# Context pieces beside light experts only, and a new order of the experts

## The chip, the cores and the metric

The kernel runs on one core of a Trainium2 chip. The metric is the device time of one execution in microseconds, as the median of several runs. Engines are named as in the profile: PE (TensorE), PEld (its weight loads), DVE (VectorE), ACT (ScalarE), POOL (GpSimd) and SP (SyncE, which here issues most of the transfers from HBM).

## What is computed

Two model blocks follow each other. The first is a mixer and a mixture of 32 experts; the second has two layers that attend jointly to 512 tokens and to a context of 256 tokens. The change touches the expert stage of the first block. Its core, cut from the reference:

```python
logits = (xf @ w_router).astype(jnp.float32) + b_router.astype(jnp.float32)
top_val, top_idx = lax.top_k(logits, TOP_K)          # 4 of 32 experts a token
...
hu = xb @ w_up[e] + b_up[e]
x_glu = jnp.minimum(hu[:, :D_FF], SWIGLU_LIMIT)
x_lin = jnp.clip(hu[:, D_FF:], -SWIGLU_LIMIT, SWIGLU_LIMIT)
act = x_glu * jax.nn.sigmoid(SWIGLU_ALPHA * x_glu) * (x_lin + 1.0)
return act @ w_down[e] + b_down[e]
```

So each expert has three matrices of 1024 x 1024 float32 values, 4 MB each: the gate half of w_up, the linear half of w_up, and w_down. The context's part of the second block's first layer does not depend on the first block:

```python
hc, gate_c = adaln(xc, mod_c)
qac, kac, vac, qbc, kbc, vbc, gc = heads_ab(hc @ w_in, *wts)
...
mixc = jnp.concatenate([oac, obc], axis=-1) * jax.nn.silu(gc)
xc = xc + gate_c * (mixc @ w_out)
```

It is therefore computed beside the experts.

## The kernel before

The experts are ranked by their number of tokens. `CAPS` gives the places of each rank: ranks 0 and 1 have two blocks (128 and 64 tokens, called T here), ranks 2 to 13 have one of 128 (heavy, H), ranks 14 to 31 one of 64 (light, L). `moe` (line 780) makes a list `order` of ranks and works through it. In iteration i it runs the gate matrix of expert i (`expert_gate`), then the w_down matrix of expert i-1 (`expert_down`), then the linear matrix of expert i (`expert_lin`). Ahead of the last it prepares the tokens of the expert after (`turn`) and the slots and the gather of the one after that (`prep`). One more iteration, i = 32, runs the last w_down.

`expert_mm` (line 1193) works on one matrix. It issues four transfers of 1 MB on SP's queue (line 1214, tile `raw`, four buffers for the whole stage). For a light expert it multiplies the float32 weights directly, 32 matmuls of 512 columns (line 1221), and ACT and DVE fold the two halves of the result afterwards (lines 1175 and 1176). For heavy and two-block experts every half of `raw` is split into a high part on ACT (line 72, `whi`) and a low part on DVE (line 73, `wlo`), in buffers of which there are four, and 48 matmuls of 512 columns follow (line 1236); a T expert has more of them for its second block. Line 1211 or 1219 starts the sums with the bias.

The context is the generator `context` (line 1476). Its 57 yields make 58 steps, here called pieces: 24 of projections and norms, 4 of queries, keys and values, 18 of attention, 8 of `w_out`, then the row normalization for the second layer and two pieces of that layer's keys and values. The matrix pieces load their weights on SP (line 1510), split them on ACT and DVE (lines 72 and 73), and run 24 matmuls of 256 columns (lines 98 to 100) each. `moe` calls `step()` behind each matrix, three times an iteration; each call lets the generator go on by one piece, until call 30, and from there three of four calls do. The order of the instructions on an engine is the order of the code with these pieces between; a scheduler then moves instructions a little.

The order before is L, then H L for ranks 13 to 2 (i = 1 to 24), then T L L (i = 25 to 27), T L L (28 to 30), and L (31). The context is used up by about i = 22. One iteration ahead of `last` (i = 23) the rest of the generator is drained, and a pool `moe3` for the token tiles of the last experts is opened in the place that the context's memory has left; `tags` names the token tiles, and `hilo` (line 1147) takes those named y and v from `moe3`.

Behind the loop the hook `after` prepares the second block (`second_start`, line 2063): gains and rows of scale factors are loaded on ACT's queue (lines 2043 to 2073), POOL makes the tables of rope gains (lines 1837 to 1844), and two weight tiles of the second block are loaded on SP (line 77). Then a branch (line 1329) skips the work for overfull experts, and `combine` (line 1376) loads the experts' rows (`y<-Yd`) and adds them; each row is normalized with its statistics on POOL (line 68) before the first matmul of the second block.

Of the kernel before, what the change touches and what calls it, by code (L numbers as in the profile page):

```python
# [13 lines left out]
BF16 = mybir.dt.bfloat16  # L14
# [7 lines left out]
P = 128  # L22
D = 1024
S = 512
NT = S // P
# [9 lines left out]
class Net:  # L35
# [737 lines left out]
    NE = 32  # L773
# [6 lines left out]
    def moe(self, mix, mods, close, x1, modd, h2d, Yd, bd, beside=(), after=None):  # L780
# [4 lines left out]
        NE = self.NE  # L785
        with ExitStack() as ctx:
# [24 lines left out]
            with c2:  # L811
                pools = self.moe_pools(c2)
                self.xg_init(pools)

                light = list(range(14, NE))
                order = [light.pop(0)]
                for r in range(13, -1, -1):
                    order += [r] + [light.pop(0) for _ in range(min(len(self.CAPS[r]), len(light)))]
                order += light

                last = min(i for i, r in enumerate(order) if len(self.CAPS[r]) > 1) - 1
                tags = []
                for i, r in enumerate(order):
                    if len(self.CAPS[r]) > 1:
                        tags.append("xz")
                    elif i >= last:
                        tags.append("v" if tags[-1] == "y" else "y")
                    elif self.CAPS[r] == (64,) and (not i or tags[-1] != "z"):
                        tags.append("z")
                    else:  # L830
                        tags.append("x")

                def prep(r, behind=None):
                    out, off = [], 0
# [29 lines left out]
                self.extra_plan(c1, tab)  # L864
                down, beside = None, iter(beside)

                cnt = [0]

                def step():
                    cnt[0] += 1  # L870
                    if cnt[0] < 30 or cnt[0] % 4:
                        next(beside, None)

                more = ExitStack()

                for i in range(NE + 1):
                    if i < NE:
                        r = order[i]
                        pk = pick[:, r : r + 1]
                        e = nc.values_load(tab["eri"][0:1, r : r + 1], engines=[mybir.EngineType.SP], min_val=0,  # L880
                                           max_val=NE - 1)
                        wu = A["w_up"][0, ds(e, 1)].rearrange("o k c -> (o k) c")
                        wd = A["w_down"][0, ds(e, 1)].rearrange("o k c -> (o k) c")
                        hs = self.expert_gate(raws, pools, tab, cur, pk, wu)
                        step()
                    if down is not None:
                        self.expert_down(raws, pools, tab, *down, Yd)
                        step()
                    if i < NE:
                        if i + 1 == last:  # L890
                            for _ in beside:
                                pass
                            pools["more"] = more.enter_context(self.pool("moe3", 1, side="right"))
                        nxt = turn(ahead, i + 1) if i + 1 < NE else None
                        ahead = prep(order[i + 2]) if i + 2 < NE else None
                        acts = self.expert_lin(raws, pools, tab, cur, hs, pk, wu)
                        down = (cur, acts, pk, wd)
                        cur = nxt
                        step()
                more.close()  # L900
                if after is not None:
                    after()
            self.moe_extra(tab, h2d, Yd)
# [194 lines left out]
    def slots(self, pools, tab, pos, rhs, cap, later=False):  # L1098
# [1 line left out]

        nc = self.nc
        t2 = pools["t2"]
        oh = t2.tile([P, NT, P], BF16, tag="oh", name="oh")
        iota = tab["iota_s"] if cap == 128 else tab["iota_d"]
        nc.vector.tensor_tensor(oh, iota[:, None, :].to_broadcast([P, NT, P]), pos.to_broadcast([P, NT, P]),
                                op=OP.is_equal)
# [40 lines left out]
    def hilo(self, pools, tag, cap, whole):  # L1147


        t2 = pools["more"] if tag in "yv" else pools["t2"]  # L1150
        x = {"whole": whole}
        if whole:
            x["f"] = t2.tile([P, KT, cap], F32, tag=tag + "h", name=tag, bufs=1)
# [1464 lines left out]
```

## Time and profile before

| what | value |
|---|---|
| median of 3 runs | 2619.11 us (2616.77 to 2623.46) |
| the profiled execution | 2624.55 us, its span 2622.8 us |
| PE busy | 2343.2 us, 89% of the span |
| PEld busy | 1594.3 us, 61% |
| DVE busy | 1661.4 us, 63% |
| ACT busy | 1150.0 us, 44% |
| POOL busy | 500.5 us, 19% |
| read from and written to HBM | 563.56 MB and 23.46 MB, 224 GB/s over the span |

The profile is of one execution. A busy PE is not PE at its peak, since the ends of matmuls are modelled; idle time of an engine that does not bound a stretch costs nothing. The expert loop runs from about 536 to 1889 us. What one change there is worth is read from its own stretch, not from the shares of the whole span. Times in all rows count from the start of the span.

### The profile page before, as it was taken

The page shows a single profiled execution, that of the slowest core. Times are in us where ns is not written, and L with a number is a line of the kernel's source. Part 1 is how long each engine was busy: PE and PEld are TensorE (multiplying, and loading weights), DVE is VectorE, ACT ScalarE, POOL GpSimd, SP SyncE. Part 2 cuts the span into 40 slices and gives each one's busy share as a digit, 9 for nine tenths or more (in the row PEclk, how much of TensorE's full clock was granted, in tenths as well). Part 3 has the DMA queues.
Part 4 walks back from the last instruction along what each step waited for, and adds up shares of the span by engine and source line. Part 5 has one row for each costly group of instructions (what it writes and reads, how often), then busy time and mean ns, then how long its engine had stood idle before and what let it go on. Part 6 is the DMA issues. An engine that isn't in the chain of part 4 may idle for free. (4 is left out here: it accounts for less than half of the span.)

```text
span 2622.8 us, 33292 instructions
## 1 busy us (share of the span) xinstructions
PE 2343.2 (89%) x12070; PEld 1594.3 (61%) x12070; DVE 1661.4 (63%) x2730; ACT 1150.0 (44%) x1948; POOL 500.5 (19%) x686
## 2 busy tenths in 40 slices
PE   4987998979999999999999989999659899999888
PEld 4864666636656555555556556454159787687766
DVE  6798564456566686667566765444286788556483
ACT  3342553224454455455445443333224478432362
POOL 4335332210010001011000000000143213232112
PEclk7998998999999999999999989999979899999999
DMA  7551204689999998898999998888962101222101
GB/s 259 180 174 65 98 17 148 239 314 322 344 335 324 333 350 298 317 331 312 346 353 341 339 336 314 296 309 303 370 223 78 40 33 33 89 76 89 67 22 41
DMA packets 207234, 580.85 MB, mean 221 GB/s; under 512 B 16739, under 2 KB 68944, under 8 KB 207066
## 3 DMA queue, kind: packets, MB, share of 16 engines
q1 hardware_dynamic: 186624, 539.33, 57.8%
q10 hardware_dynamic: 13210, 22.57, 2.5%
q0 software_dynamic: 7232, 16.79, 1.8%
q8 instruction: 96, 1.57, 0.2%
q14 instruction: 72, 0.59, 0.1%
HBM read 563.56 MB, written 23.46 MB: 224 GB/s over the span
## 5 line engine op out<-in xcount | busy, mean ns | idle before, releaser
L73 DVE TENSOR_TENSOR wlo<-raw,whi 128x1024 fp32r<-128x1024 f32 (+3 forms) x420 | 510.2, 1250 | 129.3 <-ACT whi L72 128.2
L72 ACT ACTIVATE whi<-raw 128x1024 fp32r<-128x1024 f32 (+4 forms) x439 | 462.8, 1093 | 201.0 <-PE ps L100 48.9
L1236 PE MATMUL ps<-whi,x 128*128 128x512 f32 x896 | 268.9, 412 | 12.3 <-ACT whi L72 12.3
L1176 DVE TENSOR_TENSOR fold<-ps,fold 64x512 f32<-64x512 f32 x120 | 82.0, 683 | 206.7 <-ACT fold L1175 205.0
L1236 PEld LDWEIGHTS ps<-whi,x 128*128 128x128 f32 x896 | 174.2, 197 | 61.8 <-ACT whi L72 21.4
L1221 PE MATMUL ps<-raw,z 128*64 128x512 f32 x768 | 187.6, 609 | 3.8 <-DMA raw<-in_w_up_dram 3.8
L1142 POOL DMA_INDIRECT xg<-h2d,si x34 | 40.6, 1193 | 652.2 <-issue 199.8
L1175 ACT ACTIVATE fold<-ps 64x512 f32<-64x512 f32 x120 | 71.1, 593 | 205.5 <-PE ps L1221 178.7
L1236 PE MATMUL ps<-wlo,x 128*128 128x512 f32 x448 | 154.1, 426 | 7.1 <-DVE wlo L73 6.6
L1221 PE MATMUL ps<-raw,a 128*64 128x512 f32 x576 | 139.0, 608 | 4.1 <-DMA raw<-in_w_down_dram 3.4
L73 DVE TENSOR_TENSOR PTl<-tp,PTh 128x512 fp32r<-128x512 f32 (+1 forms) x178 | 111.6, 639 | 46.3 <-ACT PTh L72 44.6
L1914 ACT ACTIVATE pt<-sp,st 128x768 f32<-128x768 f32 (+4 forms) x160 | 110.2, 690 | 57.7 <-DVE st L1908 24.2
L1908 DVE TENSOR_REDUCE st<-sp 128x1 f32<-128x768 f32 (+5 forms) x144 | 108.3, 753 | 42.6 <-PE sp L449 17.2
L1236 PE MATMUL ps<-whi,a 128*128 128x512 f32 x448 | 129.9, 402 | 1.1 <-ACT whi L72 1.1
L72 ACT ACTIVATE PTh<-tp 128x512 fp32r<-128x512 f32 (+1 forms) x178 | 97.4, 559 | 70.6 <-PE tp L1952 55.6
L1293 POOL DMA_INDIRECT Yd<-y,si x34 | 38.5, 1133 | 390.2 <-ACT y L1291 388.4
L1952 PE MATMUL tp<-ident,pt 128*128 128x128 f32 x648 | 107.2, 278 | 3.2 <-DVE QS L490 1.3
L73 POOL TENSOR_TENSOR wlo<-raw,whi 128x2048 fp32r<-128x2048 f32 (+2 forms) x19 | 76.5, 4033 | 148.2 <-ACT whi L72 132.9
L1236 PEld LDWEIGHTS ps<-wlo,x 128*128 128x128 f32 x448 | 81.4, 197 | 36.2 <-DVE wlo L73 20.2
L1236 PEld LDWEIGHTS ps<-whi,a 128*128 128x128 f32 x448 | 84.1, 190 | 21.4 <-ACT whi L72 1.6
L1221 PEld LDWEIGHTS ps<-raw,z 128*64 128x64 f32 x768 | 46.7, 136 | 79.6 <-issue 70.3
L1952 PEld LDWEIGHTS tp<-ident,pt 128*128 128x128 f32 x648 | 78.9, 142 | 22.7 <-issue 3.6
(728 smaller groups left out, 5400.9 us busy)
## 6 DMA issues: line engine op xcount, KB each, us to landing
raw<-in_w_up_dram SPq DMA_DIRECT2D x256, 1024.0 KB
raw<-in_w_down_dram SPq DMA_DIRECT2D x128, 1024.0 KB
raw<-in_w_ada_dram SPq DMA_DIRECT2D x24, 1024.0 KB
raw<-in_mod_w_dram SPq DMA_DIRECT2D x24, 1024.0 KB
raw<-in_cd_w_in_dram SPq DMA_DIRECT2D x13, 1024.0 KB
raw<-in_w_in_dram SPq DMA_DIRECT2D x10, 1024.0 KB
raw<-in_ab_w_out_dram SPq DMA_DIRECT2D x16, 512.0 KB
y<-Yd SPq DMA_DIRECT2D x16, 512.0 KB
```

Source lines behind the costliest of these rows:

```text
L72: self.nc.scalar.activation(hi, src, AF.Copy)
L73: (eng or self.nc.vector).tensor_sub(lo, src, r32(hi))
L1142: nc.gpsimd.indirect_dma_start(out=xg[:cap, :], out_offset=None, in_=h2d, in_offset=bass.IndirectOffsetOnAxis(ap=ii[:cap, 0:1], axis=0), b ...
L1175: self.nc.scalar.activation(h, ps[j][64:128, :], AF.Copy)
L1176: self.nc.vector.tensor_add(h, ps[j][0:64, :], h)
L1221: nc.tensor.matmul(ps[j][64 * k : 64 * k + 64, :], x[:, 2 * q + k, :], raw[:, k, j * 512 : j * 512 + 512], start=q == 0 and k == 1, stop=q ...
L1236: nc.tensor.matmul(ps[j], a, w[:, j * 512 : j * 512 + 512], start=False, stop=kk == KT - 1 and n == len(seq) - 1)
L1293: nc.gpsimd.indirect_dma_start(out=out, out_offset=bass.IndirectOffsetOnAxis(ap=ii[:, 1:2], axis=0), in_=y, in_offset=None, bounds_check=4 ...
L1908: nc.vector.reduce_max(nm, s[0] if m == 1 else sp[:, : m * n].rearrange("p (x k) -> p x k", k=n), axis=AX.X, negate=True)
L1914: nc.scalar.activation(pt[:, :n], s[x], AF.Exp, bias=nm[:, x : x + 1], accum_out=u["st"][:, 1, c + x : c + x + 1])
L1952: nc.tensor.transpose(tp[:, b, :], u["pt"][i, b][:, k * P : (k + 1) * P], self.ident)
```

## The change

The new order has two light experts first: L L, then H L for six ranks (i = 2 to 13), T L L (14 to 16), H L three times (17 to 22), T L L (23 to 25), H L three times (26 to 31). `step()` lets the context go on only if expert i is light, at each of its three calls; the count of calls is gone. In 31 iterations this makes 52 pieces. The other six (the last two of `w_out`, the row normalization, two pieces of keys and values, and the end of the generator) are drained at i = 31, between the w_down of expert 30 and the linear matrix of expert 31. The third pool is gone, the token tiles are named x, z and y and all lie in the pool of the others, and the one-hot tile `oh` has one buffer in place of two. Lines behind the edited ones are ten lower in the changed code (1226 is 1236 before).

```diff
--- before.py
+++ after.py
@@ -813,22 +813,18 @@
                 self.xg_init(pools)
 
                 light = list(range(14, NE))
-                order = [light.pop(0)]
-                for r in range(13, -1, -1):
-                    order += [r] + [light.pop(0) for _ in range(min(len(self.CAPS[r]), len(light)))]
-                order += light
-
-                last = min(i for i, r in enumerate(order) if len(self.CAPS[r]) > 1) - 1
-                tags = []
-                for i, r in enumerate(order):
-                    if len(self.CAPS[r]) > 1:
+                order = [light.pop(0), light.pop(0)]
+                for r in [*range(13, 7, -1), 1, *range(7, 4, -1), 0, *range(4, 1, -1)]:
+                    order += [r] + [light.pop(0) for _ in self.CAPS[r]]
+                two = [len(self.CAPS[r]) > 1 for r in order] + [False]
+                tags = ["x"]
+                for i, r in enumerate(order[1:], 1):
+                    if two[i]:
                         tags.append("xz")
-                    elif i >= last:
-                        tags.append("v" if tags[-1] == "y" else "y")
-                    elif self.CAPS[r] == (64,) and (not i or tags[-1] != "z"):
-                        tags.append("z")
+                    elif two[i - 1] or two[i + 1]:
+                        tags.append("y")
                     else:
-                        tags.append("x")
+                        tags.append("z" if self.CAPS[r] == (64,) else "x")
 
                 def prep(r, behind=None):
                     out, off = [], 0
@@ -864,14 +860,10 @@
                 self.extra_plan(c1, tab)
                 down, beside = None, iter(beside)
 
-                cnt = [0]
-
                 def step():
-                    cnt[0] += 1
-                    if cnt[0] < 30 or cnt[0] % 4:
+
+                    if i < NE and self.CAPS[order[i]] == (64,):
                         next(beside, None)
-
-                more = ExitStack()
 
                 for i in range(NE + 1):
                     if i < NE:
@@ -887,17 +879,15 @@
                         self.expert_down(raws, pools, tab, *down, Yd)
                         step()
                     if i < NE:
-                        if i + 1 == last:
+                        if i + 1 == NE:
                             for _ in beside:
                                 pass
-                            pools["more"] = more.enter_context(self.pool("moe3", 1, side="right"))
                         nxt = turn(ahead, i + 1) if i + 1 < NE else None
                         ahead = prep(order[i + 2]) if i + 2 < NE else None
                         acts = self.expert_lin(raws, pools, tab, cur, hs, pk, wu)
                         down = (cur, acts, pk, wd)
                         cur = nxt
                         step()
-                more.close()
                 if after is not None:
                     after()
             self.moe_extra(tab, h2d, Yd)
@@ -1100,7 +1090,7 @@
 
         nc = self.nc
         t2 = pools["t2"]
-        oh = t2.tile([P, NT, P], BF16, tag="oh", name="oh")
+        oh = t2.tile([P, NT, P], BF16, tag="oh", name="oh", bufs=1)
         iota = tab["iota_s"] if cap == 128 else tab["iota_d"]
         nc.vector.tensor_tensor(oh, iota[:, None, :].to_broadcast([P, NT, P]), pos.to_broadcast([P, NT, P]),
                                 op=OP.is_equal)
@@ -1147,7 +1137,7 @@
     def hilo(self, pools, tag, cap, whole):
 
 
-        t2 = pools["more"] if tag in "yv" else pools["t2"]
+        t2 = pools["t2"]
         x = {"whole": whole}
         if whole:
             x["f"] = t2.tile([P, KT, cap], F32, tag=tag + "h", name=tag, bufs=1)
```

On PE, at the end of a heavy expert's gate matrix and the start of the w_down of the light expert ahead of it, there stands before (`acc` and `b0`, `b1` are the context's, `ps` and `x` or `a` the expert's):

```order
L1236 MATMUL ps_5309<-whi_5391,x_5189 128x512
L1236 MATMUL ps_5310<-whi_5391,x_5189 128x512
L98 MATMUL acc_5448<-whi_5490,b0_4391 128x256
L99 MATMUL acc_5448<-wlo_5491,b0_4391 128x256
L1221 MATMUL ps_5450<-raw_5452,a_5254 64x512 x2
L1221 MATMUL ps_5451<-raw_5452,a_5254 64x512 x2
L100 MATMUL acc_5448<-whi_5490,b1_4392 128x256
```

There a piece of the context is mixed into the start of the light matrix. After, at a place of the same kind:

```order
L1226 MATMUL ps_5471<-whi_5553,x_5351 128x512
L1226 MATMUL ps_5472<-whi_5553,x_5351 128x512
L1211 MATMUL ps_5573<-raw_5575,a_5416 64x512 x2
L1211 MATMUL ps_5574<-raw_5575,a_5416 64x512 x2
L1201 LDWEIGHTS pick_4130
L1201 MATMUL ps_5643<-bu_3499,pick_4130 128x512
```

The light matrix follows the heavy one with nothing of the context between; only the bias of the next matrix stands there.

On PE, in the w_down of the last expert, before:

```order
L1273 MATMUL tp_14872<-ident_69,ln_14869 128x128 x4
L1221 MATMUL ps_14878<-raw_14880,a_14863 64x512 x2
L1221 MATMUL ps_14879<-raw_14880,a_14863 64x512 x2
L1221 MATMUL ps_14878<-raw_14888,a_14863 64x512 x2
L1221 MATMUL ps_14879<-raw_14888,a_14863 64x512 x2
L1221 MATMUL ps_14878<-raw_14894,a_14863 64x512 x2
```

The expert's matmuls stand alone there. After (`s4` is a row of the context, `tp` its transposes in the row normalization):

```order
L1211 MATMUL ps_14875<-raw_14885,a_14860 64x512 x2
L1211 MATMUL ps_14876<-raw_14885,a_14860 64x512 x2
L336 MATMUL tp_14706<-ident_69,s4_14703 128x128 x4
L1211 MATMUL ps_14875<-raw_14891,a_14860 64x512 x2
L98 MATMUL acc_14722<-whi_14725,b0_14669 128x256
L99 MATMUL acc_14722<-wlo_14726,b0_14669 128x256
L1211 MATMUL ps_14876<-raw_14891,a_14860 64x512 x2
L336 MATMUL tp_14713<-ident_69,s4_14703 128x128 x4
```

The context's row normalization and its keys now stand between the last expert's matmuls.

On ACT, around the last w_down of the loop, before (`cg`, `scr_`, `shr_` and `g2` are gains and rows of scale factors for the second block):

```order
L1175 ACTIVATE fold_14864<-ps_14836 64x512
L2069 DMA cg_14920<-in_mla_cq_gain_2_dram 128x256
L2070 DMA cg_14920<-in_mla_ckv_gain_2_dram 128x256
L2043 DMA scr__14923<-modd_94 128x1024
L1166 ACTIVATE a_14863<-tp_14872 128x512
L2046 DMA shr__14926<-modd_94 128x1024
L2073 DMA g2_14928<-modd_94 128x1024
L1175 ACTIVATE fold_14906<-ps_14878 64x512
```

These transfers are issued between the last folds. After, behind the branch that ends the loop:

```order
L1319 COMPARE_AND_BRANCH
L1319 UNCONDITIONAL_BRANCH
L1789 DMA kvckv_102<-KV_14720 128x2x256
L2059 DMA cg_14916<-in_mla_cq_gain_2_dram 128x256
L2060 DMA cg_14916<-in_mla_ckv_gain_2_dram 128x256
L2033 DMA scr__14919<-modd_94 128x1024
L2036 DMA shr__14922<-modd_94 128x1024
L2063 DMA g2_14924<-modd_94 128x1024
L2068 DMA rp_14937<-in_rope_dram 128x4x192
```

The store of the context's keys comes first, and all loads of the second block's gains stand behind it; POOL's rope tables and SP's loads of the first two weight tiles have moved behind the branch too.

## Rows read from the trace of the kernel before

**Rows 1.** The page's first line: span and instruction count.

```profile
span 2622.8 us, 33292 instructions
```

**Rows 2.** Table by stretch: length, busy by engine, PEclk, DMA share, GB/s.

```profile
566.10:1581.50 1015.40, 955.98 (x4573) 581.28 (x4573) 671.37 (x1098) 509.36 (x735) 90.13 (x114) 0.98 0.94 332
...
1509.40:1528.80 19.40, 15.70 (x67) 11.14 (x65) 11.18 (x23) 7.48 (x9) 2.70 (x3) 0.82 0.93 332
1581.50:1708.60 127.10, 117.26 (x526) 68.21 (x526) 61.85 (x110) 47.30 (x62) 8.40 (x9) 0.97 0.84 305
...
1836.70:1889.00 52.30, 40.45 (x167) 12.48 (x166) 9.64 (x16) 7.88 (x13) 11.65 (x40) 0.97 1.03 405
```

**Rows 3.** Grouped lines, 566.1 to 1581.5: busy, mean ns, idle before and releaser.

```profile
L1221 PE MATMUL ps<-raw,z 128*64 128x512 f32 x728 | 176.7, 605 | 0.0
...
L99 PE MATMUL acc<-wlo,b 128*128 128x256 f32 x128 | 36.5, 288 | 4.8 <-DVE wlo L73 4.8
```

**Rows 4.** Grouped lines of PE, 1581.5 to 1836.7.

```profile
L1221 PE MATMUL ps<-raw,v 128*64 128x512 f32 x104 | 26.8, 628 | 9.4 <-DMA raw<-in_w_up_dram 9.4
```

**Rows 5.** Timeline of PE: start, us, instruction; where heavy and light matrices begin.

```profile
1528.80 1.08 PE L1221 MATMUL ps<-raw,a 128*64 128x512 f32 x4
...
1539.69 1.22 PE L1236 MATMUL ps<-whi,x 128*128 128x512 f32 x2 [1.07 <-ACT whi L72]
...
1554.25 1.94 PE L1221 MATMUL ps<-raw,y 128*64 128x512 f32 x8
...
1566.59 0.73 PE L1236 MATMUL ps<-whi,a 128*128 128x512 f32 x2
...
1579.55 1.94 PE L1221 MATMUL ps<-raw,y 128*64 128x512 f32 x8
...
1590.76 1.20 PE L1236 MATMUL ps<-whi,x 128*128 128x512 f32 x2
```

**Rows 6.** Timeline of SP: first w_up transfer of experts 2 and 10.

```profile
615.12 0.38 SPq L1214 DMA_DIRECT2D raw<-in_w_up_dram  x1
...
957.45 0.38 SPq L1214 DMA_DIRECT2D raw<-in_w_up_dram  x1
```

**Rows 7.** Timeline of ACT behind a light matrix.

```profile
1563.99 0.59 ACT L1175 ACTIVATE fold<-ps 64x512 f32<-64x512 f32 x1 [0.27 <-PE ps L1221]
...
1565.10 1.99 ACT L72 ACTIVATE whi<-raw 128x1024 fp32r<-128x1024 f32 x2
```

**Rows 8.** Timelines of SP, POOL and PE from the last w_down on.

```profile
1868.13 8.97 SPq L1214 DMA_DIRECT2D raw<-in_w_down_dram  x4
1879.18 3.38 SPq L77 DMA_DIRECT2D raw<-in_ab_w_in_dram  x2
...
1868.84 0.75 POOL L1838 TENSOR_TENSOR rg0a<-rp,gn 128x256 f32<-128x256 f32 x1
...
1879.90 1.47 POOL L1844 TENSOR_TENSOR rg3b<-rp,gn 128x16 f32<-128x16 f32 x8
...
1912.32 1.02 POOL L68 TENSOR_SCALAR st<-st 128x1 f32<-128x1 f32 x1 [19.89 <-DMA y<-Yd]
...
1880.09 8.92 PE L1221 MATMUL ps<-raw,a 128*64 128x512 f32 x32 [0.75 <-ACT a L1166]
...
1919.61 0.57 PE L98 MATMUL ps<-whi,hTh 128*128 128x272 f32 x1
```

**Rows 9.** Timelines of DVE, ACT and POOL at the context's end, and one one-hot.

```profile
1501.03 0.29 DVE L1826 TENSOR_TENSOR KV<-KV,gn 128x128 f32<-128x128 f32 x1
...
1501.35 0.38 ACTq L1799 DMA_DIRECT2D kvckv<-KV  x1
...
1504.41 0.47 ACTq L1850 DMA_DIRECT2D gn<-in_mla_k_gain_dram  x1
...
1509.63 0.73 POOL L1852 TENSOR_SCALAR gn<-gn 128x64 f32<-128x64 f32 x1 [8.54 <-DMA gn<-in_gqa_q_gain_dram]
...
1523.57 0.68 DVE L1105 TENSOR_TENSOR oh<-iota_d,pos 128x512 bf16<-128x512 f32 x1
```


## The prediction

> **What bounds the kernel now.** I read the slices of the page first, then tables by stretch of the expert loop, then the timelines of single engines at a few places. The span is 2622.8 us [rows 1]. The expert loop fills 536 to 1889 of it, and the change touches only this loop and what follows it. Of 1015.4 us in which twelve heavy-light pairs run, PE is busy for 955.98, and the DMA engines carry 332 GB/s at a share of 0.94 [rows 2]. Both could be the bound. The grouped lines decide: the light matmuls there have no idle time ahead of them at all, and the context's matmuls wait 4.8 us in all for the low half of a split, made on DVE [rows 3]. No transfer stands ahead of PE in this stretch. So PE's queue, fed by the splits, sets the pace where context pieces run.
>
> In the two stretches with a two-block expert and two or three light ones no context is left. In the first, PE is busy 117.26 of 127.1 us, the transfers take 0.84 [rows 2], and the light matmuls wait for w_up [rows 4]. Two resources are thus used in turns: PE is overfull where the pieces are, and has about 10 us to spare in each of these stretches.
>
> **The heavy-light pairs.** Before, a piece follows each of six matrices of a pair; after, only the three steps of the light expert's turn yield one. I need the price of a pair without pieces and the price of one piece. The only matrices without a piece lie at 1528 to 1591, around the last pair [rows 5]. The starts give light matrices of 1539.69-1528.80 = 10.89, 1566.59-1554.25 = 12.34 and 1590.76-1579.55 = 11.21, mean 11.48; heavy ones of 1554.25-1539.69 = 14.56 and 1579.55-1566.59 = 12.96. The 14.56 comes right behind a stretch in which the granted clock was 0.82 [rows 2], so I take 12.96. A bare pair is 3 x (12.96 + 11.48) = 73.3 us; its bounds are 3 x (12.96 + 10.89) = 71.6 and 3 x (14.56 + 12.34) = 80.7.
>
> Four pairs with six pieces each ran from 615.12 to 957.45, 85.6 each [rows 6]. A piece then costs (85.6 - 73.3)/6 = 2.05 us, with bounds of 0.8 and 2.3. That is less than its matmuls: 24 of 256 columns, by half the 1.94/8 us of a 512-column one [rows 5], are an estimated 2.9 us. The difference is the hand-over from light to heavy, where ACT first does the folds (until 1564.58) and splits the first weights only at 1565.10 [rows 7]; a piece fills that hole in PE.
>
> A pair after the change is 73.3 + 3 x 2.05 = 79.4 us, the last with two pieces 77.4. Twelve make 11 x 79.4 + 77.4 = 951, against 1015.4: **-64 us**. By the bounds the same line gives -74 and -18 (80.7 + 3 x 0.8 = 83.1 a pair). The stall of 19.4 us at 1509.4, when the separate pool was opened and the context drained [rows 2], lies inside the 1015.4 and is not counted again. Transfers do not stand against it: 332 GB/s over 1015.4 us are 337 MB, of which the experts' weights, 24 transfers of 1.05 MB a pair, are 302; the 35 MB left are those of some 55 pieces, and 35 pieces bring about 22. Then 324 MB in 951 us are 341 GB/s, and the last stretch of before reached 405 [rows 2].
>
> **The two-block stretches.** Each now carries six pieces. Six at 2.05 cost 12.3 us in full; nothing, if all goes into the waits of PE. PE's matmul work of six pieces, 17 us, is more than the 9.8 us that are free, so I take half: 6 us each, **+12** (bounds 0 and 25).
>
> **The front and the last light expert.** One light expert moves from the end to the front. At the end its turn, from 1836.7 to the last w_down issues at 1868.13 [rows 8], took 31.4 us; it goes. At the front there is one more turn with three pieces, 3 x 11.48 plus part of 6.2, 38 us. **+6.6** (3 to 9).
>
> **The drain.** Six pieces are left for the last light expert: two w_out pieces, the row normalization, two pieces of keys, and the close. Before, these were hidden in a dense loop; now they run with the last w_up and w_down, and PE has nothing behind them. Four matmul pieces are 4 x 2.9 = 11.6 us on PE. The normalization is a chain of ACT, POOL, DVE and PE; the same chain at the start of the second block takes from 1912.32 to 1919.61, 7.3 us [rows 8]. Sum about **+18.5**. The bounds are 8.2 (four at 2.05, with the chain covered by the last matmuls) and 30 (nothing covered, some of it at the lower clock).
>
> **The transition.** The order of ACT puts the store of the keys, and then ten other transfers, behind the branch that ends the loop. They wait for the small DVE operations of the last norm; in before the store was issued at 1501.35, right behind the last of them [rows 9]. Six issues take until 1504.88, ten about 6 us; the gains reached POOL at 1509.63 [rows 9], 4.7 us later; the rope tables, which ran from 1868.84 to 1881.4 under the last matmuls [rows 8], take 12.5 us plus 1 for scaling the gains. With 3 us for the norm this makes 27 us from the last matmul until POOL comes to the row statistics, against 1912.32-1889.01 = 23.3 in before, where the last matmuls started at 1880.09 and took 8.92 [rows 8]. That is +4. The first two weights of the second block, issued at 1879.18 before [rows 8], now stand on SP behind ten loads of rows; I put their landing and split at +5. Together **+9** (0, if the rows' transfers, for which POOL waited 19.89 us [rows 8], cover all; 20, if the two chains add).
>
> **The rest costs nothing.** The one-hot tile with a single buffer waits for PE's four small matmuls on it, for which DVE's copy waits anyway; that copy is the cover, and without it at most 0.68 us for each of 34 blocks [rows 9] would be lost, 23 us. The token tiles alternate in two names and are free one expert earlier than needed; the third pool's opening falls away with its stall, counted above.
>
> **The sum.** -64 + 12 + 6.6 + 18.5 + 9 = -18. The profiled execution took 2624.55 us (its span plus 1.8), 5.4 above the median of 2619.11, so it becomes about 2606.5, and the median **2601 us**.
>
> A rule that speaks against the change: the Trainium skill, "Perfetto Trace Analysis", section "Identifying the Most-Contended Engine", holds that the matmul busy share is no measure of headroom, because matmuls are pipelined, and wants TensorE judged by its utilization and by the busy share of the weight loads. The weight loads are busy 581.28 of 1015.4 us here [rows 2], which by that rule leaves room; the trace agrees only in part, as no matmul there waits for a transfer.
>
> **Rivals.** *A, more is hidden.* The bare pair is 71.6, the two-block stretches swallow their pieces, the drain lies half beside the last matmuls: -74 + 0 + 5 + 14 + 5 = -50, 2569 us. For it: PE's free 10 us per stretch; against: the drain has no work behind it.
>
> *B, the tail takes the gain.* The pairs gain 64, but drain and transition cost 28 + 18 in place of 27.5: about 0, 2619 us. For it: the order shows keys, gains and rope tables in one chain through four engines; against: POOL waited for rows until 1912.32 in any case.
>
> *C, the heavy matrix is no quicker alone (slower).* What limits it is the hand-over of folds and splits on ACT and DVE, so the bare pair is 80.7, as the 14.56 and the 12.34 say, and a piece was nearly free, 0.8. A pair becomes 83.1, the pairs gain 18, and 5 + 5 + 18.5 + 9 = 37.5 is paid behind: +19, 2638 us. It decides from a pair above 84.6 - 46/12 = 80.8 us. For it: the hole before 1565.10 [rows 7]; against: 12.96 and 11.21, measured one after the other.
>
> *D, PE has room and moving the pieces gains nothing.* Pieces cost the same wherever they stand, so only some 7 us of the stall at 1509.4 are gained and 46 are paid: +39, 2658 us. Against it: six pieces a pair cost 12 us over the bare matrices [rows 5, 6]. This is what the rule named above would lead to.
>
> **How the numbers follow.** Forecast 0.54 (2578 to 2613), A 0.10, B 0.17, C 0.14, D 0.05. A measurement of this kernel can tell about 0.3%, 7.9 us, from no change: 2611 to 2627 is the same. Faster: nearly all of the forecast, A and a third of B, 0.64; the same: most of B and the edge of the forecast, 0.18; slower: C and D, less C's near edge, with B's far one, 0.18. For 8 in 10 the range leaves out half of A, D and the far half of C: 2570 to 2636.
>
> **What would show it.** In the profile after, twelve pairs of 78.6 to 80.5 us between first w_up issues show the pair's price right; 83 shows C. Two-block stretches of 131 to 137 show the half cover. From the last w_down issue to the first matmul of the second block before took 1919.61-1868.1 = 51.5 us; about 65 is foreseen with part of the drain ahead of it, and above 80 shows B. POOL's row statistics that wait for rows, not for rope tables, would make the transition free. The forecast is wrong if the pairs come out above 80.8, or if PE in them begins to wait for transfers.

## The result and the profile after

The changed kernel takes 2631.37 us (median of 12 runs, 2625.05 to 2638.53), the kernel before 2618.98 (12 runs). The ratio is 1.0054, with a 95% interval of 1.0041 to 1.0066: slower by about 12 us, where a time 18 us shorter was forecast.

The profiled execution of the changed kernel has a span of 2629.7 us, 6.9 above that of before [rows 1]. Its engines do the same work: PE has as many instructions and nearly the same busy time.

```profile
span 2629.7 us, 33318 instructions
...
PE 2341.1 (89%) x12070; PEld 1589.8 (60%) x12070; DVE 1659.8 (63%) x2730; ACT 1154.6 (44%) x1948; POOL 491.4 (19%) x686
```

The loop of the changed kernel, cut where the first w_up transfers of its experts are issued: two light experts, six heavy-light pairs, a two-block stretch, three pairs, a two-block stretch, two pairs, one heavy expert, the last light expert up to the last matmul, and the way to the first matmul of the second block. Columns as in [rows 2].

```profile
533.10:609.80 76.70, 63.52 (x308) 26.66 (x307) 28.77 (x61) 18.93 (x30) 6.39 (x10) 0.93 0.91 312
609.80:1080.40 470.60, 445.88 (x2074) 263.86 (x2074) 293.50 (x434) 228.75 (x294) 32.68 (x33) 0.99 0.96 352
1080.40:1212.90 132.50, 127.52 (x585) 78.24 (x586) 80.84 (x153) 60.35 (x90) 8.82 (x11) 0.99 0.85 314
1212.90:1463.20 250.30, 233.67 (x1110) 137.18 (x1111) 175.52 (x316) 132.07 (x214) 25.92 (x42) 0.97 0.90 320
1463.20:1597.20 134.00, 128.60 (x607) 75.51 (x603) 72.11 (x129) 58.75 (x96) 11.58 (x22) 0.99 0.83 303
1597.20:1754.30 157.10, 144.78 (x656) 84.57 (x657) 97.65 (x146) 76.11 (x96) 12.56 (x15) 0.98 0.96 352
1754.30:1794.10 39.80, 37.00 (x178) 21.06 (x178) 21.16 (x25) 16.93 (x21) 1.40 (x2) 1.00 0.91 322
1794.10:1873.60 79.50, 70.65 (x363) 45.77 (x362) 44.49 (x53) 32.01 (x42) 2.89 (x6) 0.94 0.75 280
1873.60:1923.40 49.80, 2.21 (x11) 1.62 (x9) 20.86 (x46) 3.63 (x9) 15.69 (x44) 0.54 0.71 248
```

The first profile of before stood 5.4 us above its median, while this one stands at its own. So the kernel before was profiled a second time (span 2617.8, time 2619.54). The same table of that second profile: first light expert, twelve pairs, last light expert, way to the second block.

```profile
532.10:566.60 34.50, 22.21 (x99) 6.85 (x100) 15.57 (x38) 8.04 (x13) 4.32 (x8) 0.85 0.88 284
566.60:1575.60 1009.00, 952.77 (x4573) 578.90 (x4573) 670.43 (x1098) 509.31 (x735) 90.10 (x114) 0.98 0.94 334
...
1828.70:1881.40 52.70, 41.55 (x167) 13.07 (x166) 9.69 (x16) 7.89 (x14) 11.65 (x40) 0.94 1.03 405
1881.40:1911.60 30.20, 1.90 (x9) 1.50 (x9) 21.81 (x25) 9.72 (x17) 5.41 (x4) 0.54 0.89 321
```

| stage | before, first profile | before, second | after | change (first, second) | forecast |
|---|---|---|---|---|---|
| start of the loop | 536.0 | 532.1 | 533.1 | -2.9, +1.0 | 0 |
| front (one light turn before, two after) | 30.1 | 34.5 | 76.7 | +46.6, +42.2 | +38 |
| pairs (12 before; 11 and the last heavy turn after) | 1015.4 | 1009.0 | 917.8 | -97.6, -91.2 | -100 |
| two-block stretches, both | 255.2 | 253.1 | 266.5 | +11.3, +13.4 | +12 |
| last light expert to the last matmul | 52.3 | 52.7 | 79.5 | +27.2, +26.8 | +22.6 |
| way to the second block | 30.6 | 30.2 | 49.8 | +19.2, +19.6 | +9 |
| the rest | 703.2 | 706.2 | 706.3 | +3.1, +0.1 | 0 |
| sum | | | | +6.9, +11.9 | -18 |

The forecast column regroups the terms of the prediction: -64 for the pairs, less the 35.5 us of a light turn with its two pieces that stands in the last light expert's row, is -100; the front's +38 stands without the turn that goes at the end; 22.6 is the drain's 18.5 and the two pieces' 4.1. Against the second profile, which is the typical one, the sum is +11.9, as the medians say.

The pairs came out at 878.0/11 = 79.8 us, and the last heavy turn at 39.8: the loop's middle does what was foreseen. The loss is at both ends, most of all behind the loop. Timelines of DVE, ACT, POOL, SP and PE there, in the changed kernel (dots mark left-out rows and the next engine):

```profile
1882.88 0.29 DVE L1816 TENSOR_TENSOR KV<-KV,gn 128x128 f32<-128x128 f32 x1
...
1893.73 0.69 DVE L2034 TENSOR_SCALAR scr__14919<-scr__14919 128x1024 f32<-128x1024 f32 x1 [4.94 <-DMA scr__14919<-modd]
...
1883.20 0.38 ACTq L1789 DMA_DIRECT2D kvckv<-KV  x1
...
1893.73 0.34 ACTq L1840 DMA_DIRECT2D gn<-in_gqa_q_gain_dram  x1
...
1898.03 0.44 ACTq L1840 DMA_DIRECT2D gn<-in_mla_k_gain_dram  x1
...
1904.13 0.19 ACT L2045 ACTIVATION_READ_ACCUMULATOR ht<-xt 128x1 f32 x1
...
1903.02 0.39 POOL L1842 TENSOR_SCALAR gn<-gn 128x64 f32<-128x64 f32 x1 [28.73 <-DMA gn<-in_mla_k_gain_dram]
...
1917.60 0.19 POOL L68 TENSOR_SCALAR st<-st 128x1 f32<-128x1 f32 x1
...
1840.83 6.24 SPq L1204 DMA_DIRECT2D raw<-in_w_down_dram  x4
...
1902.95 14.98 SPq L77 DMA_DIRECT2D raw<-in_ab_w_in_dram  x2
...
1923.35 0.60 PE L98 MATMUL ps<-whi,hTh 128*128 128x272 f32 x1 [0.83 <-ACT whi L72]
```

The rows show one chain. The last keys are normalized at 1883.17, 9.6 us behind the last matmul. Their store is issued at once, and the ten loads behind it take until 1898.47. POOL waits 28.73 us for the gains and comes to the row statistics at 1917.60, where in before [rows 8] it had long made its tables and waited only for rows. Here the rows are not what it waits for: ACT is done with them at 1904.32, 30.7 us behind the last matmul, and POOL is busy with the tables for another 13.3 us.

The ten loads take so long because half of them wait. By the semaphores in the trace, five of the ten are issued within 0.02 us of the landing of an earlier transfer that used the same semaphore. The first gain is such a case: it is issued at 1893.73, when the row of scale factors lands for which DVE waits 4.94 us in the rows above. POOL's first operation needs that gain, whose load lands at 1902.93.

The second of the two weight loads is issued 15 us behind the first, when POOL is done with the tables, whose memory it takes over. SP's own waits from 1870 to 1930 put it down to POOL:

```profile
SPq L77 <- POOL st L68: 14.1, 1, 14.1
```

### The profile page after: what moved, and what is told of

The parts are those of the page before. It is cut to its first block, busy times and chain, and to the rows that moved or that the text cites. A ratio compares the mean times of both kernels' runs of the same rounds, so it can differ in the third digit from the quotient of the medians.

```text
span 2629.7 us, 33318 instructions
## 1 busy us (share of the span) xinstructions
PE 2341.1 (89%) x12070; PEld 1589.8 (60%) x12070; DVE 1659.8 (63%) x2730; ACT 1154.6 (44%) x1948; POOL 491.4 (19%) x686
## 5 line engine op out<-in xcount | busy, mean ns | idle before, releaser
L73 DVE TENSOR_TENSOR wlo<-raw,whi 128x1024 fp32r<-128x1024 f32 (+2 forms) x420 | 511.3, 1251 | 127.7 <-ACT whi L72 126.9
L1226 PE MATMUL ps<-whi,x 128*128 128x512 f32 x896 | 260.7, 402 | 7.1 <-ACT whi L72 6.8
L1211 PE MATMUL ps<-raw,z 128*64 128x512 f32 x832 | 203.2, 608 | 1.8 <-DMA raw<-in_w_up_dram 1.7
L1226 PEld LDWEIGHTS ps<-whi,x 128*128 128x128 f32 x896 | 168.5, 191 | 57.9 <-ACT whi L72 19.1
L1166 DVE TENSOR_TENSOR fold<-ps,fold 64x512 f32<-64x512 f32 x120 | 81.9, 683 | 145.1 <-ACT fold L1165 143.7
L1211 PEld LDWEIGHTS ps<-raw,z 128*64 128x64 f32 x832 | 52.0, 136 | 89.1 <-issue 78.2
L1226 PEld LDWEIGHTS ps<-wlo,x 128*128 128x128 f32 x448 | 78.5, 191 | 40.8 <-DVE wlo L73 27.3
L1942 PEld LDWEIGHTS tp<-ident,pt 128*128 128x128 f32 x648 | 78.9, 142 | 22.1 <-issue 2.8
```

Of the source, the lines that this page charges most:

```text
L73: (eng or self.nc.vector).tensor_sub(lo, src, r32(hi))
L1166: self.nc.vector.tensor_add(h, ps[j][0:64, :], h)
L1211: nc.tensor.matmul(ps[j][64 * k : 64 * k + 64, :], x[:, 2 * q + k, :], raw[:, k, j * 512 : j * 512 + 512], start=q == 0 and k == 1, stop=q ...
L1226: nc.tensor.matmul(ps[j], a, w[:, j * 512 : j * 512 + 512], start=False, stop=kk == KT - 1 and n == len(seq) - 1)
L1942: nc.tensor.transpose(tp[:, b, :], u["pt"][i, b][:, k * P : (k + 1) * P], self.ident)
```

## The experiments

All kernels run the whole computation; they differ in the order and in the place of buffers. Each diff is against the changed kernel. A table by stage is that of one profiled execution, which can lie some us off the median of its kernel; where that is more than 5 us it is said.

**The order alone.** The old rule for the pieces is put back, everything else stays as changed.

```diff
+                cnt = [0]
+
                 def step():
-
-                    if i < NE and self.CAPS[order[i]] == (64,):
+                    cnt[0] += 1
+
+                    if cnt[0] < 30 or cnt[0] % 4:
                         next(beside, None)
```

> The changed kernel with the old rule for the context's pieces (three an iteration until call 30, then three of four), the new order kept. The context is then used up near i = 22. Theory 1 (the loss lies at the end, in the drain beside the last expert and in the chain of key store, gains and rope tables behind the loop): the stretch from the first w_up issue of the last expert to the first matmul of the second block falls from 129 us back to about 83, and the whole is near 2600 us, clearly faster than before, since the new order alone removes the stall of the pool. Rival (the order itself is at fault, two light experts first and two-block ones in the middle): 2625 us or more, with the end as short as before.

Measured: 2617.75 us, ratio to before 0.9994 (0.9978 to 1.0010). The table by stage of this kernel, the first six pairs, the last two, the last light expert, and the way to the second block:

```profile
610.30:1121.80 511.50, 480.49 (x2324) 292.63 (x2326) 346.79 (x583) 264.24 (x393) 40.67 (x56) 0.99 0.93 330
1653.40:1803.10 149.70, 135.85 (x576) 74.40 (x575) 88.98 (x129) 69.06 (x84) 9.95 (x9) 0.98 0.97 360
1837.80:1893.10 55.30, 49.31 (x203) 25.39 (x202) 25.02 (x29) 19.45 (x24) 0.97 (x1) 0.94 0.90 335
1893.10:1919.20 26.10, 1.96 (x11) 1.59 (x9) 17.11 (x18) 5.25 (x9) 4.51 (x4) 0.54 0.75 286
```

The end is as short as before (81.4 us from the last expert's first transfer, 129.3 after the change). So the order is not what lengthens the end. It brings no gain either, which is a miss of the expected 2600. That number counted on the stall of the pool, 19.4 us; but PE was busy for 15.70 of them [rows 2], and the heavy matrix that fills them is only 6.4 us longer than the bare one of 12.96. Pairs with six pieces take 511.5/6 = 85.3, those with none 149.7/2 = 74.9, as in the kernel before.

**The context done before the last expert.** Nine more pieces beside early heavy experts.

```diff
-                    if i < NE and self.CAPS[order[i]] == (64,):
+                    if i < NE and (self.CAPS[order[i]] == (64,) or i in (2, 4, 6)):
```

> The changed kernel with nine more pieces, three beside each of the heavy experts at i = 2, 4 and 6, so that the context ends before the last expert. Theory 1: three pairs grow from 78.4 to about 85 us (+18), the last expert loses its eight pieces and its drain, rope tables and weights of the second block move back under the last matmuls; 129 us at the end become 83 to 88; the whole is 2598 to 2604 us. Rival (only the drain's own work was in the way, and the chain behind the loop stays): the end is about 105 us and the whole about 2622 us.

Measured: 2614.51 us, ratio 0.9988 (0.9973 to 1.0003); that is 17 us below the changed kernel. The last light expert and the way to the second block:

```profile
1817.70:1871.90 54.20, 48.20 (x203) 25.22 (x202) 25.10 (x30) 19.55 (x24) 0.98 (x1) 0.97 1.00 370
1871.90:1900.70 28.80, 1.93 (x11) 1.49 (x9) 21.85 (x25) 9.62 (x17) 5.39 (x4) 0.57 0.86 316
```

The end shrinks from 129.3 to 83.0, as theory 1 said. The three pairs that got the nine pieces take 255.7 us in place of 237.2, the 18 that were set. But the last expert's first transfer comes at 1817.7 in place of 1794.1, 23.6 us later: the pairs behind, with other pieces in them now, grew too. So what the drain gives back goes into the pairs; what is won is the chain behind the loop. The profiled execution (2607.88 us) is the quickest of the ten, 6.6 below the median, and the median is 10 us above the 2598 to 2604 expected.

**Pieces beside heavy experts only.**

```diff
-                    if i < NE and self.CAPS[order[i]] == (64,):
+                    if i < NE and self.CAPS[order[i]] != (64,):
```

> The changed kernel with the three pieces of a pair beside the heavy (and two-block) expert in place of the light one; 16 pieces are left for the drain, so only the pairs at i = 2 to 13 are compared. If a piece costs the same wherever it stands, a pair stays near 78.4 us. If the light expert's matrices hide pieces better, as the change's rule supposes, a pair is 81 us or more. If the hand-over after a light matrix is where a piece is free, it is again the pair with pieces beside heavy that is longer or equal, never shorter.

Measured: 2653.85 us in one run, with its 16 pieces in the drain and 84.5 us to the second block. The two turns at the front and the first six pairs:

```profile
533.80:564.40 30.60, 21.64 (x99) 6.50 (x99) 10.50 (x29) 5.35 (x9) 3.57 (x6) 0.83 0.85 264
564.40:596.20 31.80, 27.00 (x119) 9.74 (x118) 9.22 (x22) 6.70 (x11) 1.49 (x2) 0.97 1.03 400
596.20:1085.90 489.70, 456.44 (x2116) 274.04 (x2115) 295.50 (x439) 230.91 (x297) 35.74 (x36) 0.97 0.96 341
```

These pairs take 81.6 us, 3 more than beside light experts, but the three pairs from 17 on take 78.2 and not 83.4, and the last two 83.1 and not 78.5. Over all eleven it is 80.95 against 79.8: on the mean of this one run the neighbour's kind is worth 0.4 us a piece. Single stretches differ by more in both directions, and other pieces stand in them. The front shows more: without pieces its two turns take 62.4 us, with five 76.7, 2.9 us a piece. That is as much as the prediction's estimate of a piece's matmuls. PE is busy 48.64 us in the bare turns and 63.52 with the five pieces, 14.9 more, so PE's own work accounts for all of the 14.3 us, and nothing of a piece is hidden there.

**The bare loop.** The whole context runs at the first step.

```diff
-                    if i < NE and self.CAPS[order[i]] == (64,):
-                        next(beside, None)
+                    for _ in beside:
+                        pass
```

> The changed kernel with the whole context run at its first step, ahead of the second expert, so that the loop behind it is bare. It gives the price of a bare pair: 73.3 us by the prediction, 71.6 to 80.7 by its bounds; from 78.4 with three pieces that makes 1.7 us a piece at 73.3. If a bare pair is 76 us or more, a piece beside light experts costs under 0.8 us and the pair is bound by something else, such as the transfers (25.2 MB a pair). The two-block stretches should take 127 us bare.

Measured: 2648.08 us in one run. The stretches that follow the context: the first two-block stretch, three pairs, the second two-block stretch, and two pairs:

```profile
1203.60:1328.90 125.30, 116.44 (x514) 67.77 (x513) 65.07 (x107) 51.11 (x69) 12.62 (x8) 0.97 0.92 334
1328.90:1551.80 222.90, 202.35 (x876) 111.71 (x876) 136.39 (x206) 104.11 (x127) 16.14 (x13) 0.98 0.97 358
1551.80:1681.10 129.30, 119.19 (x514) 69.39 (x514) 60.16 (x98) 46.99 (x61) 8.23 (x8) 0.95 0.85 309
1681.10:1829.30 148.20, 133.73 (x576) 73.79 (x575) 88.94 (x129) 68.84 (x84) 10.03 (x8) 0.99 0.97 360
```

A bare pair, cut at the first transfers, is 74.3 and 74.1 us. The 73.3 of the prediction was right to 1 us. The two-block stretches are 125.3 and 129.3 bare, so twelve pieces cost 266.5-254.6 = 11.9 us in the changed kernel, 1.0 each: the only cheap place. All 58 pieces in one place cost just 31 to 35 us more than spread as before (1383.6 from the first transfer to the last expert's last matmul, against 1352.4 and 1348.6).

**The drain one expert earlier.**

```diff
-                        if i + 1 == NE:
+                        if i + 2 == NE:
                             for _ in beside:
```

> The changed kernel with the drain one expert earlier, in the turn of the last heavy expert (i = 30), so that the context ends about 60 us before the last matmul of the loop. Eight pieces then stand in one place beside a heavy matrix. Theory 1 (the chain behind the loop costs, not the drain as such): the turn of i = 30 grows from 39.9 to 55 to 60 us, the stretch from the first w_up issue of expert 31 to the last expert matmul falls from 75.6 to about 53, and from there to the first matmul of the second block from 53.6 to about 30; together -23 to -30, the whole 2602 to 2610 us. Rival (the drain costs the same wherever it is serial, and the chain only moves with it): the whole stays above 2620.

Measured: 2632.56 us, ratio 1.0048 (1.0024 to 1.0073): no better than the change, a clear miss. The profiled execution is one of two quick ones among the six (2621.95 us; the four others took 2632.51 to 2635.25), so what the slower ones lost beyond its stages no trace shows. In it, the way to the second block fell from 49.8 to 38.8, and the heavy turn grew by 12, but the last expert still took 73.1. The timelines of this kernel (PE, then DVE, ACT and POOL) show why:

```profile
1868.11 1.11 PE L1263 MATMUL tp<-ident,ln 128*128 128x128 f32 x4 [11.01 <-DVE ln L1260]
...
1866.30 0.69 DVE L2034 TENSOR_SCALAR scr__14919<-scr__14919 128x1024 f32<-128x1024 f32 x1 [8.28 <-DMA scr__14919<-modd]
1866.91 0.42 DVE L1259 TENSOR_SCALAR ln<-fold 128x512 f32<-128x512 f32 x1
...
1853.20 1.00 ACTq L2033 DMA_DIRECT2D scr__14919<-modd  x1
...
1887.56 1.06 POOL L1283 DMA_INDIRECT Yd<-y,si  x1 [0.15 <-POOLq L1319]
```

The chain has moved ahead into the last expert, and its waits now stand in the queues that the expert needs. DVE's addition to the row of scale factors waits 8.28 us for a load that was issued at 1853.20 and came 13 us later, among the experts' weights; the expert's own `ln` stands behind it on DVE, and PE waits 11.01 us for that. POOL scatters the last expert's rows only at 1887.56, behind the rope tables, 7 us after `y` was ready. So it is not enough to end the context one expert earlier.

**The rope tables in memory of their own.** Only the place and the point of issue change; the drain stays.

```diff
-        with self.pool("ab5", 1, side="right") as cp:
+        pre["rg"] = []
+
+        def tables(cp):
             rp = cp.tile([P, NT, 192], F32, name="rp")
...
+                tb = c3.enter_context(self.pool("ab5", 1))
...
                     self.adaln_tile(hp, tp_p, xt, rows, hTh, hTl, t, True)
+                    if t == 0:
+                        pre["tables"](tb)
```

> The changed kernel with the drain where it is, but with the rope tables of the second block in memory of their own, which the context does not occupy: their loads are then issued on ACT ahead of the store of the keys, and the first two weights on SP behind four row loads in place of eleven. Nothing in the loop changes. Theory 1: the drain stays (75.6 us from the first w_up issue of expert 31 to the last expert matmul), the way from there to the second block shrinks from 53.6 to 33 to 40 us, and the whole by 14 to 20, to 2611 to 2617 us. If the loads of rows and the small norms are what is waited for, the gap stays at 50 or more and the whole above 2627 us.

Measured: 2620.35 us, ratio 1.0015 (0.9999 to 1.0032), 11 us below the changed kernel. The last expert stays at 78.9 us, the way behind it is 39.0 in place of 49.8:

```profile
1798.00:1876.90 78.90, 70.87 (x363) 45.70 (x362) 44.38 (x52) 32.00 (x42) 2.93 (x6) 0.94 0.76 282
1876.90:1915.90 39.00, 1.94 (x10) 1.57 (x8) 23.02 (x52) 9.62 (x19) 19.96 (x43) 0.55 0.86 290
```

So over half of the 19 us behind the loop were the tables and the weights that waited for them; the run moves both their memory and their place in the order, and does not tell these two apart. What is left is in the same kernel's timelines of ACT, DVE and POOL:

```profile
1886.46 0.38 ACTq L1789 DMA_DIRECT2D kvckv<-KV  x1
...
1892.67 0.76 ACTq L2033 DMA_DIRECT2D scr__14919<-modd  x1
...
1900.13 0.77 DVE L2034 TENSOR_SCALAR scr__14919<-scr__14919 128x1024 f32<-128x1024 f32 x1 [4.52 <-DMA scr__14919<-modd]
1902.56 1.66 DVE L73 TENSOR_TENSOR wlo<-raw,whi 128x544 fp32r<-128x544 f32 x2 [1.67 <-ACT whi L72]
1904.14 1.23 DVE L1384 TENSOR_TENSOR y<-y,g 128x1024 f32<-128x1024 f32 x1
...
1902.94 6.30 POOL L1834 TENSOR_TENSOR rg3b<-rp,gn 128x16 f32<-128x16 f32 x8
...
1910.14 0.36 POOL L68 TENSOR_SCALAR st<-st 128x1 f32<-128x1 f32 x1 [0.90 <-ACT ht L2045]
```

The row of scale factors is still loaded behind the store of the keys. DVE's addition to it waits 4.52 us for that load, a split of the weights behind it waits 1.67 us more, and the sum of the first rows goes on only at 1904.14. With the rows of scale factors in memory of their own too the rest might go; that was not tried.

**No pieces in front, some beside the two-block experts.**

```diff
-                    if i < NE and self.CAPS[order[i]] == (64,):
+                    if 1 < i < NE and (self.CAPS[order[i]] != (128,) or i in (2, 4, 6)):
```

> No pieces beside the first two light experts; three each beside the two-block experts and the heavy ones at i = 2, 4 and 6 instead, so that the context ends before the last expert. Theory 2 (beside the first two light experts the transfers are the bound, and five pieces cost 14 us there): the first two turns fall from 76.3 to 62 us against the run with pieces to i = 6; the two-block stretches grow by 4 to 6 us each; the whole is 3 to 7 us below that run, near 2608 to 2611 us. Rival (a piece costs about 2 us anywhere): no difference from that run, 2614 us.

Measured: 2613.61 us, ratio 0.9978 (0.9962 to 0.9994). The front fell to 62.3 us, the size that theory 2 gave; its reason, that the transfers are the bound there, is not shown, since PE's own work accounts for the difference (above). The whole is no quicker than the run with pieces to i = 6 (2614.51, and the two intervals overlap), a miss of the 2608 to 2611. The first two-block stretch, with nine pieces, took 148.0 us, where the run with pieces to i = 6 has 131.1 with six: the 14 us of the front were spent again. The second one took 136.8 with nine pieces and 136.9 in that run with six, so nine pieces are not dear in every two-block stretch.

**Two pieces in every iteration.** The rule of the neighbour is dropped, and the pieces are spread evenly.

```diff
+                cnt = [0]
+
                 def step():
-
-                    if i < NE and self.CAPS[order[i]] == (64,):
+                    cnt[0] += 1
+
+                    if 0 < i < NE and cnt[0] % 3:
                         next(beside, None)
```

> The changed kernel with two pieces in every iteration from the second on, whatever the expert, so that the context ends at i = 29. By the prices so far (a bare pair 74.2 us, some 2 to 2.5 us a piece) a pair with four pieces takes 82 to 84 us, the two-block stretches with six 131 to 135, the end is as short as in the kernel before (82 to 84 us from the first w_up issue of expert 31 to the second block), and the whole is 2611 to 2617 us, the same as with nine pieces beside early heavy experts. If the choice of the neighbour matters (light experts hide pieces better), it is above 2620 us; if an even spread hides more, below 2608 us.

Measured: 2607.21 us, ratio to before 0.9950 (0.9932 to 0.9968): faster than the kernel before by 12 us and than the changed one by about 24. Front, six pairs, the first two-block stretch, the last light expert and the way behind it:

```profile
532.60:601.60 69.00, 51.96 (x221) 16.39 (x221) 24.06 (x55) 14.76 (x24) 6.52 (x10) 0.90 0.95 340
601.60:1093.00 491.40, 465.35 (x2208) 284.24 (x2209) 307.99 (x479) 239.99 (x313) 34.57 (x35) 0.99 0.94 341
1093.00:1228.00 135.00, 128.85 (x595) 75.62 (x595) 85.59 (x163) 62.51 (x104) 10.78 (x20) 1.00 0.85 307
1818.80:1875.40 56.60, 51.68 (x206) 28.50 (x204) 25.61 (x30) 20.06 (x25) 12.88 (x25) 0.91 0.96 352
1875.40:1903.80 28.40, 1.88 (x10) 1.44 (x9) 21.79 (x25) 9.62 (x17) 5.38 (x4) 0.59 0.85 317
```

Pairs with four pieces take 81.9 us, this two-block stretch with six 135, and the end is 85 us, each within 1 us of what was expected. Nothing is left for the drain. The median is 4 us below the expected 2611 to 2617 and just under the 2608 set for an even spread that hides more; but the profiled execution (2612.81 us) lies 5.6 above it, so no stage shows where these last us are won. The Trainium skill, "Perfetto Trace Analysis", section "Optimization Strategy", says that where the most-contended engine changes over a kernel, interleaving its regimes may help. The even spread can be read as such an interleaving, and this run is in line with it, with 0.5%.

## Why the prediction was wrong

**The bound and the pairs: right.** No wait for a transfer stands ahead of PE in the first six pairs, and the pairs stay below the 80.8 that was the sign of a wrong forecast. A bare pair is 74.1 to 74.9 us in two kernels, against 73.3; a pair with three pieces 79.8 against 79.4. The piece's price of 2.05 holds from three to six pieces: (79.8-74.2)/3 = 1.9, (82.3-74.2)/4 = 2.0 over the eleven pairs of the even spread (905.6 us in all), (85.3-74.2)/6 = 1.85. Rival C, that a heavy matrix alone is no quicker, is out. These signs looked at the pairs only, which is why they stayed silent while the whole came out slower.

**The two-block stretches: right,** +11.3 and +13.4 against +12.

**The front: the step that prices its turn at 38 us was too low.** It took the price of a light turn at the end, and 2 us a piece. The runs show 62.4 us for two bare turns and 2.9 us for each of five pieces: nothing of a piece is hidden there, where the price of 2 us supposed that nearly a third is. The two turns cost +42 to +47 in place of +38. Taken by the first profile alone, 30.1 us for one turn was also a low base; the second profile has 34.5.

**The drain: the mechanism right, the size low.** +27 for eight pieces, where 22.6 were set (its two parts, 11.6 and 7.3, make 18.9 and not 18.5), 3.4 us a piece, the most expensive place of all. The chain of the row normalization, priced at 7.3 us, is there. PE's waits in the last light expert's row begin with it:

```profile
PE tp L336 <- DVE s L1543: 7.5, 1, 7.5
```

**The transition: the step that failed.** It was sized at +9, at most 20, and is +19.4. The chain of keys, gains and tables was named there in full, but two of its links were sized too small. Three us were set for the norm, from no row; 9.6 passed from the last matmul until the keys were ready, because two tiles are normalized by fifteen small DVE operations each, one behind the other, and DVE passes the branch between two of them (2.7 us). Six us were set for ten loads, in proportion to six issues of before that did not wait; from the store to the last gain they took 1883.20 to 1898.47, 15.3, as five of them waited for the landing of earlier transfers. The landing, 4.6, and POOL's part, 14.6, were near the 4.7 and 13.5 of the text. The links are 44 us in place of 27. The other +5, for the first two weights, did not show at the first matmul: PE waits 0.83 us there for a split.

The run with the tables in their own memory took 11 us of this away, the runs with the context done early all of it. From the last w_down issue (1840.83) to the first matmul of the second block it is 82.5 us, above the 80 that was named as the sign of rival B. B had 46 us for drain and transition, and 46 it was; but B was put at 0.17, on the ground that POOL waited for rows in any case. That cover failed: the rows were ready at 1904.32, and POOL came to them 13.3 us later.

**The basis.** The sum was made against a profile that was 5.4 us above the median. The largest difference between the two profiles lies in the stretch that the change shortens (1009.0 against 1015.4 for the pairs), so 6.4 of the 64 us of the pairs were that profile's own. Against the second profile the forecast is off by 30 us: 10.6 of them lie in the transition, 8.8 in the pairs, these 6.4 among them, about 4 each in the front and the drain, and 2.5 elsewhere.

**What the change does, then.** It does not hide the context better. A piece costs about 2 us beside a heavy or a light matrix alike. Of the 56 that stood in the pairs 21 are moved out; each costs 1 us again beside the two-block stretches' experts, 2.9 at the front and 3.4 at the end. The loop up to its last matmul is 8.8 to 12.5 us shorter, where 27 were forecast, and the chain behind it costs 19. Rival D, that PE has room and moving pieces gains nothing, is out: it had some 7 us from the pairs, and they gave 56 to 62 of the 64. The rule named beside it, of the Trainium skill, "Perfetto Trace Analysis", section "Identifying the Most-Contended Engine", would have seen room in weight loads that are busy 263.86 of 470.6 us in the pairs. The runs show little of that room: each piece costs 1.85 us or more there, of an estimated 2.9 us of matmuls.

**What stays open.** Why the first two-block stretch took 148 us with nine pieces, while the second took 136.8, was not separated by kind of piece. That waiting issues, and not something else, made the ten loads slow is read from one trace; no run changed it alone. Nor was it tried whether the old order with an even spread is as quick as the new one.

## What to carry to other kernels

When work beside a loop is moved, price it at the place to which it goes, and count what must wait for its end: here the store, the gains, the memory that it frees, and every queue on which these stand. In these runs the side work that feeds the next stage had to end well before the loop, neither in its last turn nor in the one ahead of it. Where a piece costs the same beside every neighbour, a rule that favours one neighbour has nothing to win and leaves a rest for the end; of the spreads tried the even one was the quickest.

## What the runs showed of the hardware

A load of one row took 13 us from its issue on ACT (1853.20) to its use on DVE (1866.30) in a run in which the transfers moved 378 GB/s in just these 13 us, at a share of 0.97. The operation that waited for it held up the expert's `ln` behind it on DVE, and PE with it for 11.01 us. Five of ten loads behind the loop of the changed kernel were issued only when an earlier transfer of the same semaphore had landed. Eight small POOL operations that take 1.47 us in before [rows 8] took 6.30 in the run with the early tables, at a time when DVE split weights (1902.56 to 1910.4); whether that is the cause was not tried.
